# Seven of eight column groups of an up-projection by Strassen's seven block products

## The chip, the core and the metric

The kernel runs on one core of a Trainium2 chip. Its engines work side by side, each through its own queue in order: TensorE (PE, with its weight loads listed as PEld), VectorE (DVE), ScalarE (ACT), GpSimd (POOL) and SyncE (SP, which issues most transfers). Transfers run on the core's 16 DMA engines. The metric is the device time of one launch in microseconds.

## The reference

Two transformer blocks are computed for 256 tokens in float32, one after the other. The changed part is the feed-forward part of the first block:

```python
u = rms_norm(h, norm_mlp_w[l])                                    # 256 x 2048
h = h + jnp.square(jax.nn.relu(u @ w_up[l])) @ w_down[l]          # w_up 2048 x 8192, w_down 8192 x 2048
```

Before it stands a mixer (w_in, two kinds of attention, two branch projections, w_out), behind it a norm and the second block (w_in_2, two more kinds of attention, w_out_2).

## The kernel before

Every projection is a `Job`: 512 columns of one weight matrix times all 256 tokens, with two accumulators in PSUM, one for each half of the tokens (128 rows). TensorE multiplies in the fast format fp32r. To keep float32 accuracy each operand is split in two: a high part, rounded to fp32r, and a low part, the rest. Three of the four products are added: high x high, high x low, low x high. The activations lie transposed in `op_` tiles (`ops[name, g]`: two parts, 4 k tiles of 128, 256 tokens and 16 more columns), for `v` (the normed input of w_up) four tiles, for `h0` to `h3` (the squared relu of 2048 columns of w_up each) four tiles each. `xpose_split` makes them: four transposes on TensorE into a PSUM tile `sp`, the high part on ScalarE (L119), the low part on VectorE (L120), twice per tile.

`run_stream` is the loop over all weights. It cuts each job into pieces of 4 k tiles (512 rows of the weight, 1 MB, `raw`, three buffers) and each piece into two halves. `issue` loads a piece by SP (L241); `prep_hi` makes the high part `wh` of a half on ScalarE (L261, four buffers), three halves ahead; `prep_lo` the low part `wl` on VectorE (L275, three buffers), two halves ahead, and after a piece's second half issues the load that takes its buffer. `multiply` (L295; L293 for jobs with keys) then runs 12 matmuls of 512 columns for a half: two k tiles, two token halves, three products. At a job's last half `evac` empties the accumulators. Generators in `post` and `bg` hold the rest of the work (splits, scans, attention), and `gap` lets them go on by a step in the middle and at the end of each half. Nothing is reordered: each engine executes in the order in which this code is written.

For the feed-forward part 16 jobs of w_up and 16 of w_down alternate in groups of four: four of w_up make `h{q}`, four of w_down add its product to the residual `xres` (tiles `res`). `ev_up` takes relu on ScalarE, with the token's norm factor `r2` as scale (L721), and squares on VectorE (L722). `ev_down` adds to `res` on VectorE (L730). During the last group of w_up `prep2` loads and prepares the tables of the second block.

Of the kernel before, what the change touches and what calls it, by code (L numbers as in the profile page):

```python
# [8 lines left out]
F32 = mybir.dt.float32  # L9
F32R = mybir.dt.float32r  # L10
# [11 lines left out]
HI_AHEAD, LO_AHEAD, N_HI, N_LO = 3, 2, 4, 3  # L22
# [5 lines left out]
def two_blocks_kernel(  # L28
# [27 lines left out]
    raw_p = ctx.enter_context(tc.tile_pool(name="raw", bufs=3))  # L56
# [73 lines left out]
    def xpose_split(src, name, g, colscale=None, one=None):  # L130
# [74 lines left out]

    class Job:
# [3 lines left out]
        def __init__(self, w, r0, c0, name, groups, evac, keys=False):  # L210
            self.w, self.r0, self.c0, self.name = w, r0, c0, name
            self.groups = list(range(groups)) if isinstance(groups, int) else groups
            self.evac, self.keys = evac, keys
            self.nk, self.nc = (8, 256) if keys else (4, NCH)

        def pieces(self):
            if self.keys:
                return [(self, g * 512, ((g, range(4)), (g + 1, range(4)))) for g in self.groups[::2]]
            return [(self, g * 512, ((g, (0, 1)), (g, (2, 3)))) for g in self.groups]

    jobs = []

    def run_stream():
        pieces = [p for j in jobs for p in j.pieces()]
        halves = [(pi, h) for pi in range(len(pieces)) for h in range(2)]
        raws, whl = {}, {}

        def issue(pi, between=None):
            if pi >= len(pieces):
                return  # L230
            j, r, _ = pieces[pi]
            t = raw_p.tile([P, j.nk, j.nc], F32, tag="raw", name=nm("raw"))
            src = j.w[j.r0 + r:j.r0 + r + j.nk * P, j.c0:j.c0 + j.nc].rearrange("(k p) c -> p k c", p=P)
            if pi == 0:
                cuts = (0, 1, 2, 4)
            elif pi == 1:
                cuts = (0, 2, 4)
            else:
                cuts = (0, j.nk)
            for a, b in zip(cuts, cuts[1:]):  # L240
                nc.sync.dma_start(out=t[:, a:b, :], in_=src[:, a:b, :])  # L241
                if between is not None:
                    between(b)
            raws[pi] = t

        def half_of(i):
            pi, h = halves[i]
            j = pieces[pi][0]
            n = j.nk // 2
            return j, raws[pi][:, n * h:n * h + n, :]  # L250

        def prep_hi(i):
            if i >= len(halves):
                return
            j, t = half_of(i)
            wh = wh_p.tile([P, j.nk // 2, j.nc], F32R, tag="wh", name=nm("wh"))
            for k in ((0, 1), (1, 2)) if i < 2 else ((0, j.nk // 2),):
# [6 lines left out]
        def prep_lo(i):  # L264
            if i >= len(halves):
                return
            pi, h = halves[i]
            j, t = half_of(i)
            wh = whl[i][0]
            wl = whl[i][1] = wl_p.tile([P, j.nk // 2, j.nc], F32R, tag="wl", name=nm("wl"))  # L270
            for k in ((0, 1), (1, 2)) if i < 2 else ((0, j.nk // 2),):
# [4 lines left out]
            if h == 1:  # L276
                del raws[pi]
                issue(pi + 3)
                if 2 <= pi < 6:
                    load_x(pi - 2)  # L280

        def multiply(i, acc, t, kk):

            (pi, h), (wh, wl) = halves[i], whl[i]
            j, _, parts = pieces[pi]
            g, kts = parts[h]
            xt, k = ops[j.name, g], kts.index(kk)
            sl = slice(t * P, (t + 1) * P)
# [1009 lines left out]
```

## Time and profile before

| | |
|---|---|
| median of 3 runs | 1949.76 us (1949.54 to 1949.89) |
| profiled execution | 1949.31 us, of which the span from first to last instruction is 1947.5 us |
| TensorE | 1933.1 us busy, 99%, 9456 matmuls |
| VectorE | 1092.6 us, 56% |
| ScalarE | 899.6 us, 46% |
| GpSimd | 49.1 us, 3% |
| DMA | 344.88 MB, mean 177 GB/s |

TensorE's matmuls are pipelined, so one is listed with some 395 ns although the next starts some 232 ns later; the distance between starts is what counts. VectorE and ScalarE instructions that follow one another directly overlap a little too. "Idle before" an instruction is put down to what ended that wait. Where one transfer waits for a buffer, the queue of the engine that issues it is listed (SPq).

### The profile page before, as it was taken

The numbers are of one execution on the slowest core, as the hardware profiler recorded it, in microseconds if no ns is written. First come the engines' busy times: TensorE is split into PE (matmuls) and PEld (weight loads), VectorE is DVE, ScalarE is ACT, GpSimd is POOL, SyncE is SP. The second block draws the span as 40 slices with busy tenths as digits, with TensorE's granted clock in tenths as the row PEclk, the third lists the DMA queues.
The fourth block names the chain that finished last, engine by engine and source line by source line (L and its number), as shares of the span: only waits on it lengthen the run. The fifth ranks groups of instructions, "written<-read, shape, count | busy, mean of one in ns | idle before, by whom it ended". The sixth has DMA issues, their size and how long they took to land.

```text
span 1947.5 us, 23970 instructions
## 1 busy us (share of the span) xinstructions
PE 1933.1 (99%) x9456; PEld 1592.7 (82%) x9456; DVE 1092.6 (56%) x1526; ACT 899.6 (46%) x1267; POOL 49.1 (3%) x85
## 2 busy tenths in 40 slices
PE   9999999999999999999999999999999999999997
PEld 7888887878888888888888888888888999978886
DVE  5666655554446655555555545545566566666554
ACT  6444344364444445443444344435455444556542
POOL 0000010000000000000000000000000010001000
PEclk9999999999999999999999999999999999999999
DMA  8445464545555556555665665566555444444553
GB/s 311 152 153 170 153 197 159 173 148 180 184 191 184 184 180 195 176 192 182 187 196 183 195 182 185 186 184 211 177 188 179 159 151 136 140 151 149 176 180 123
DMA packets 183489, 344.88 MB, mean 177 GB/s; under 512 B 5888, under 2 KB 28416, under 8 KB 183376
## 3 DMA queue, kind: packets, MB, share of 16 engines
q1 hardware_dynamic: 180816, 336.48, 53.0%
q0 software_dynamic: 1696, 5.65, 0.9%
q8 instruction: 74, 1.21, 0.3%
q10 hardware_dynamic: 864, 1.21, 0.2%
q14 instruction: 39, 0.32, 0.0%
HBM read 341.23 MB, written 2.10 MB: 176 GB/s over the span
## 4 chain that ended last, share of the span: by engine, by line
PE 98%; DMA 1%; DVE 0%; ACT 0%; issue 0%; SPq 0%; DVEq 0%; POOLq 0%; POOL 0%; ACTq 0%
PE acc L295 84%; PE acc L293 6%; PE sp L142 2%; PE sp L501 1%; DMA raw<-in_w_in_dram 1%; PE sp L1090 1%; PE sp L1002 0%; PE sp L654 0%; PE sp L523 0%; PE sp L1042 0%; PE sp L1022 0%; PE sp L1023 0%; PE sp L1112 0%; PE sp L1111 0%; PE sp L667 0%
## 5 line engine op out<-in xcount | busy, mean ns | idle before, releaser
L275 DVE TENSOR_TENSOR wl<-raw,wh 128x1024 fp32r<-128x1024 f32 (+1 forms) x634 | 771.2, 1219 | 455.9 <-PE acc L295 370.9
L261 ACT ACTIVATE wh<-raw 128x1024 fp32r<-128x1024 f32 (+1 forms) x634 | 667.0, 1055 | 671.2 <-PE acc L295 634.9
L295 PE MATMUL acc<-wh,op_u 128*128 128x512 f32 x1408 | 463.2, 399 | 1.7 <-ACT wh L261 1.7
L295 PE MATMUL acc<-wh,op_v 128*128 128x512 f32 x1024 | 327.0, 395 | 0.0
L295 PE MATMUL acc<-wh,op_h 128*128 128x512 f32 x1024 | 324.0, 394 | 0.0
L295 PEld LDWEIGHTS acc<-wh,op_u 128*128 128x128 f32 x1408 | 264.4, 188 | 62.9 <-ACT wh L261 2.3
L295 PE MATMUL acc<-wl,op_u 128*128 128x512 f32 x704 | 277.8, 395 | 0.8 <-DVE wl L275 0.8
L295 PEld LDWEIGHTS acc<-wh,op_h 128*128 128x128 f32 x1024 | 192.3, 188 | 44.1
L295 PEld LDWEIGHTS acc<-wh,op_v 128*128 128x128 f32 x1024 | 192.3, 188 | 43.5
L295 PE MATMUL acc<-wl,op_h 128*128 128x512 f32 x512 | 201.8, 394 | 0.0
L295 PE MATMUL acc<-wl,op_v 128*128 128x512 f32 x512 | 201.7, 394 | 0.0
L295 PE MATMUL acc<-wh,op_z 128*128 128x512 f32 x512 | 177.0, 406 | 0.0
L295 PEld LDWEIGHTS acc<-wl,op_u 128*128 128x128 f32 x704 | 132.4, 188 | 29.7 <-DVE wl L275 2.5
L293 PE MATMUL acc<-op_z,wh 128*128 128x272 f32 x640 | 129.9, 295 | 0.0
L295 PEld LDWEIGHTS acc<-wh,op_z 128*128 128x128 f32 x512 | 96.2, 188 | 24.6 <-issue 4.3
L295 PEld LDWEIGHTS acc<-wl,op_h 128*128 128x128 f32 x512 | 96.1, 188 | 22.2
L295 PEld LDWEIGHTS acc<-wl,op_v 128*128 128x128 f32 x512 | 96.1, 188 | 21.7
L293 PEld LDWEIGHTS acc<-op_z,wh 128*128 128x128 f32 x640 | 102.4, 188 | 1.5 <-issue 1.1
L295 PE MATMUL acc<-wl,op_z 128*128 128x512 f32 x256 | 100.8, 394 | 0.0
L293 PE MATMUL acc<-op_z,wl 128*128 128x272 f32 x320 | 92.0, 288 | 0.0
L295 PE MATMUL acc<-wh,op_mg 128*128 128x512 f32 x256 | 82.1, 396 | 0.0
L295 PE MATMUL acc<-wh,op_y 128*128 128x512 f32 x256 | 80.6, 394 | 0.0
(264 smaller groups left out, 1664.6 us busy)
## 6 DMA issues: line engine op xcount, KB each, us to landing
raw<-in_w_in_dram SPq DMA_DIRECT2D x138, 1024.0 KB, 5.0
raw<-in_w_up_dram SPq DMA_DIRECT2D x64, 1024.0 KB, 5.5
raw<-in_w_down_dram SPq DMA_DIRECT2D x64, 1024.0 KB, 5.0
raw<-in_w_out_dram SPq DMA_DIRECT2D x32, 1024.0 KB, 5.0
raw<-in_w_branch_a_dram SPq DMA_DIRECT2D x8, 1024.0 KB, 5.1
raw<-in_w_branch_b_dram SPq DMA_DIRECT2D x8, 1024.0 KB, 5.1
res<-in_x_dram SPq DMA_DIRECT2D x4, 512.0 KB, 7.5
c<-in_relb_dram POOLq DMA_DIRECT2D x4, 512.0 KB, 5.7
```

Source lines behind the costliest of these rows:

```text
L142: nc.tensor.transpose(p[:, k, t * P:(t + 1) * P], src[:, t, c:c + P], ident_)
L261: act(out=wh[:, k], in_=t[:, k], func=AF.Copy)
L275: tt_(out=wl[:, k], in0=t[:, k], in1=wh[:, k].bitcast(F32), op=ALU.subtract)
L293: nc.tensor.matmul(acc, lhsT=b[:, k, sl], rhs=xt[:, a, kk, :], start=st, stop=en)
L295: nc.tensor.matmul(acc, lhsT=xt[:, a, kk, sl], rhs=b[:, k, :], start=st, stop=en)
L501: nc.tensor.matmul(p[:, 2 * h + t, :], lhsT=kq[:, h, s], rhs=qp[:, h, s], start=True, stop=True)
L1090: nc.tensor.matmul(p, lhsT=qT[64 * k:64 * k + 64, h, t * P:(t + 1) * P], rhs=kT[64 * k:64 * k + 64, h], start=True, stop=True)
```

## The change

The 8192 columns of w_up are eight units of 1024. Unit 0 is computed as before, by two jobs. For each unit from 1 to 7 the product of the 256 x 2048 input (2 x 2 blocks of 128 tokens by 1024 rows) and the unit's 2048 x 1024 weights (2 x 2 blocks b11, b12, b21, b22 of 1024 rows by 512 columns) is computed by seven block products in place of eight. Each product `p1` to `p7` has one accumulator and 8 k tiles, so four items (`Part`) of two k tiles and 6 matmuls.

The sums of activation blocks (`forms`) are made once, by `make_forms`, during unit 0: for p5, p6 and p3 in six own tiles of `c4`, and for p7 in place of a block of the `v` tiles that only unit 0 reads as it was. The sums of weight blocks are made for each item: b11 + b12 into a tile `sum` (VectorE, L342), and b12 + b22 in place (VectorE, L345). `sum` first serves p5 (as b11 + b12); when its low part is made, a DMA of POOL's queue adds b22 to it (L357), for p6; after p6 another adds b21, for p4. So b12, b22 and b21 are loaded twice. `finished` combines the products: p5, p1 and p7 are copied out of PSUM by ScalarE, the rest is added by VectorE from PSUM. `store_up` takes relu and square of the two finished 128 x 512 tiles, both on ScalarE, and appends the split.

The 28 product items of a unit alternate with the 16 w_down items of the unit before, in four rounds of `ppdppdppdpd` (p a product item, d a w_down item). w_down of unit 7 comes last, alone. A w_down job now has 1024 rows (four items) in place of 2048, 32 jobs in place of 16, and its two accumulators lie in the pool `sp`, because the products take the pool `acc`.

Loads are of two k tiles (512 KB) all through the kernel, six `raw` buffers in place of three of 1 MB, and each is issued when a buffer comes free, also after a block sum. Block sums are made four items ahead. `prep2` is split: half of it starts when unit 6 is stored, the other half (`prep2b`) when unit 7 is.

```diff
-HI_AHEAD, LO_AHEAD, N_HI, N_LO = 3, 2, 4, 3
+ADD_AHEAD, HI_AHEAD, LO_AHEAD, N_HI, N_LO, N_RAW = 4, 3, 2, 4, 3, 6
...
-    raw_p = ctx.enter_context(tc.tile_pool(name="raw", bufs=3))
+    raw_p = ctx.enter_context(tc.tile_pool(name="raw", bufs=N_RAW))
...
+        def begin(self):
+            if self.side:
+                self.accs = [ps([P, NCH]) for _ in range(2)]
+            else:
+                self.accs = [acc_p.tile([P, NKEY if self.keys else NCH], F32, tag="acc", name=nm("acc")) for _ in range(2)]
...
+    class Unit:
...
+        def items(self):
+            quarters = []
+            for names in (("p5", "p1"), ("p7", "p3"), ("p6",), ("p2",), ("p4",)):
+                for j in range(4):
+                    for n in names:
+                        quarters.append(Part(self, n, j))
+            return quarters
...
+        def finished(self, n):
+
+            a = self.bank.pop(n)
+            if n in ("p5", "p1", "p7"):
+                self.s[n] = w2([P, NCH])
+                nc.scalar.copy(out=self.s[n], in_=a)
+                return
+            s1, s5, s7 = (self.s[k] for k in ("p1", "p5", "p7"))
+            if n == "p3":
+                self.s[n] = w2([P, NCH])
+                tt_(out=self.s[n], in0=a, in1=s5, op=ALU.add)
+            elif n == "p6":
+                s6 = w2([P, NCH])
+                tt_(out=s6, in0=a, in1=s1, op=ALU.add)
+                tt_(out=s7, in0=s6, in1=s7, op=ALU.add)
+                tt_(out=s5, in0=s5, in1=s7, op=ALU.subtract)
+                tt_(out=self.s["p3"], in0=self.s["p3"], in1=s6, op=ALU.subtract)
+                self.store(1, (self.s["p3"], s5))
+            elif n == "p2":
+                tt_(out=s1, in0=a, in1=s1, op=ALU.add)
+            elif n == "p4":
+                tt_(out=s7, in0=a, in1=s7, op=ALU.add)
+                self.store(0, (s1, s7))
...
+        def adds(self):
+            u, j = self.unit, self.j
+            if self.n == "p5":
+                t = u.T["sum", j] = c4([P, 2, NCH])
+                tt_(out=t, in0=u.T["b11", j].t, in1=self.b12.t, op=ALU.add)
+                return 1
+            if self.n == "p7":
+                tt_(out=self.b12.t, in0=self.b12.t, in1=u.T["b22", j].t, op=ALU.add)
...
+        def prepared(self):
+            u, j = self.unit, self.j
+            if self.n in ("p5", "p6"):
+                more = u.load(1, 1 if self.n == "p5" else 0, j)
+                nc.gpsimd.dma_start(out=u.T["sum", j], in_=more.src, accum_op=ALU.add)
+                return 0
+            if self.n == "p4":
+                del u.T["sum", j]
+                return 0
+            return 1
...
+        def multiply(self, wh, wl):
+            u = self.unit
+            if self.j == 0:
+                u.bank[self.n] = acc_p.tile([P, NCH], F32, tag="acc", name=nm("acc"))
+            for k in range(2):
+                kt = 2 * self.j + k
+                for n, (a, w) in enumerate(((0, wh), (0, wl), (1, wh))):
+                    nc.tensor.matmul(u.bank[self.n], lhsT=form(u.name, self.n, a, kt), rhs=w[:, k, :],
+                                     start=kt == 0 and n == 0, stop=kt == 7 and n == 2)
...
+            prep_add(i + ADD_AHEAD)
             prep_hi(i + HI_AHEAD)
             prep_lo(i + LO_AHEAD)
...
+    def store_up(u):
+
+        def f(g, tiles):
+            for k, t in enumerate(tiles):
+                act(out=t, in_=t, func=AF.Relu, scale=r2[:, k:k + 1])
+                act(out=t, in_=t, func=AF.Square)
+            post.append(later(4, xpose_split([t.unsqueeze(1) for t in tiles], f"h{u}", g)))
+            if g == 0 and u >= 6:
+                bg.append(prep2() if u == 6 else prep2b())
+        return f
...
+    for u in range(1, 8):
+        parts, halves = deque(Unit(w_up, 1024 * u, "v", store_up(u)).items()), deque(down(u - 1))
+        for _ in range(4):
+            for kind in "ppdppdppdpd":
+                plan.append((parts if kind == "p" else halves).popleft())
+    plan.extend(down(7))
```

How instructions stand now is shown at three places; the number behind a name counts the tiles of that name. First TensorE inside a w_up job, before: one half item, two accumulators, 12 matmuls.

```order
L295 MATMUL acc1173_6892<-wh1167_6865,op_v1_908_5243 128x512
L295 MATMUL acc1173_6892<-wl1172_6890,op_v1_908_5243 128x512
L295 MATMUL acc1173_6892<-wh1167_6865,op_v1_908_5243 128x512 x2
L295 MATMUL acc1173_6892<-wl1172_6890,op_v1_908_5243 128x512
L295 MATMUL acc1173_6892<-wh1167_6865,op_v1_908_5243 128x512
L295 MATMUL acc1174_6893<-wh1167_6865,op_v1_908_5243 128x512
```

TensorE now, at the last item of p6 (L371, one accumulator, activations from the two parts `form1119` and `form1120`), with the w_down item behind it (L255, accumulator in `sp`):

```order
L371 MATMUL acc1555_7970<-wh1556_7977,form1119_5987 128x512
L371 MATMUL acc1555_7970<-wl1559_7990,form1119_5987 128x512
L371 MATMUL acc1555_7970<-wh1556_7977,form1120_5988 128x512
L371 MATMUL acc1555_7970<-wh1556_7977,form1119_5987 128x512
L371 MATMUL acc1555_7970<-wl1559_7990,form1119_5987 128x512
L371 MATMUL acc1555_7970<-wh1556_7977,form1120_5988 128x512
L255 MATMUL sp_1550_7950<-wh1558_7988,op_h20_1475_7615 128x512
L255 MATMUL sp_1550_7950<-wl1561_8007,op_h20_1475_7615 128x512
```

A pair `wh`, `wl` served 12 matmuls before and serves 6 in a product item. Second, VectorE at the end of a w_up job before: the square of both token halves (L722), then low parts.

```order
L275 TENSOR_TENSOR wl1002_5833<-raw985_5718,wh999_5815 128x1024
L722 TENSOR_TENSOR c4_1004_5849<-c4_1004_5849 128x512 x2
L275 TENSOR_TENSOR wl1006_5856<-raw993_5767,wh1001_5831 128x1024
L275 TENSOR_TENSOR wl1010_5874<-raw993_5767,wh1005_5854 128x1024
L120 TENSOR_TENSOR op_h01_1012_5890<-sp_1013_5891,op_h01_1012_5890 128x2x256
```

VectorE now, at the end of p6: its low parts (L490) of the next items stand before and behind the four combinations (L312 to L315), of which only the first reads PSUM.

```order
L490 TENSOR_TENSOR wl1561_8007<-raw1531_7860,wh1558_7988 128x1024
L490 TENSOR_TENSOR wl1564_8019<-raw1534_7872,wh1560_8005 128x1024
L312 TENSOR_TENSOR w2_1566_8029<-acc1555_7970,w2_1506_7764 128x512
L313 TENSOR_TENSOR w2_1544_7930<-w2_1566_8029,w2_1544_7930 128x512
L314 TENSOR_TENSOR w2_1499_7729<-w2_1499_7729,w2_1544_7930 128x512
L315 TENSOR_TENSOR w2_1547_7943<-w2_1547_7943,w2_1566_8029 128x512
L490 TENSOR_TENSOR wl1568_8040<-raw1537_7890,wh1563_8017 128x1024
L490 TENSOR_TENSOR wl1571_8058<-raw1540_7902,wh1567_8038 128x1024
```

And VectorE now at the end of a w_down job in the first round: the two sums into `res` (L958), directly behind them a block sum (L345), then low parts.

```order
L490 TENSOR_TENSOR wl1501_7733<-raw1479_7627,wh1496_7717 128x1024
L958 TENSOR_TENSOR res38_254<-sp_1473_7601,res38_254 128x512
L958 TENSOR_TENSOR res38_254<-sp_1474_7602,res38_254 128x512
L345 TENSOR_TENSOR raw1490_7679<-raw1490_7679,raw1495_7703 128x1024
L490 TENSOR_TENSOR wl1504_7754<-raw1487_7661,wh1500_7731 128x1024
```

Two instructions stood between low parts there before, and now up to four. Third, ScalarE, before at the end of a w_up job (relu straight from PSUM) and then now, at the end of p6 (relu L936 and square L937 of what VectorE combined):

```order
L261 ACTIVATE wh1167_6865<-raw1159_6801 128x1024
L721 ACTIVATE c4_1170_6883<-acc1150_6749,rstat_94 128x512
L721 ACTIVATE c4_1170_6883<-acc1151_6750,rstat_94 128x512
L261 ACTIVATE wh1171_6888<-raw1159_6801 128x1024
L261 ACTIVATE wh1175_6906<-raw1164_6835 128x1024
```

```order
L477 ACTIVATE wh1563_8017<-raw1537_7890 128x1024
L936 ACTIVATE w2_1547_7943<-w2_1547_7943,rstat_94 128x512
L937 ACTIVATE w2_1547_7943<-w2_1547_7943 128x512
L936 ACTIVATE w2_1499_7729<-w2_1499_7729,rstat_94 128x512
L937 ACTIVATE w2_1499_7729<-w2_1499_7729 128x512
L477 ACTIVATE wh1567_8038<-raw1540_7902 128x1024
L477 ACTIVATE wh1570_8056<-raw1543_7922 128x1024
```

The high part `wh1567`, of the fourth item after p6's last, now stands behind four instructions of which the first waits for VectorE's last combination.

## Rows read from the trace of the kernel before

**Rows 1.** The page: busy us (share of the span) and instructions by engine.

```profile
PE 1933.1 (99%) x9456; PEld 1592.7 (82%) x9456; DVE 1092.6 (56%) x1526; ACT 899.6 (46%) x1267; POOL 49.1 (3%) x85
```

**Rows 2.** TensorE's waits: for whom, us in total, times, longest.

```profile
PE acc L295 <- ACT wh L261: 1.7, 2, 1.2
PE sp L378 <- DVE mhalf L368: 1.1, 1, 1.1
PE acc L295 <- DVE wl L275: 0.8, 2, 0.4
```

**Rows 3.** The page: the chain that ended last, by engine.

```profile
PE 98%; DMA 1%; DVE 0%; ACT 0%; issue 0%; SPq 0%; DVEq 0%; POOLq 0%; POOL 0%; ACTq 0%
```

**Rows 4.** Windows over the feed-forward stage: busy us (instructions), granted clock, DMA share, GB/s.

```profile
core 0: us, PE busy (x) PEld busy (x) DVE busy (x) ACT busy (x) POOL busy (x), PEclk, DMA share, GB/s
692.00:783.00 91.00, 91.00 (x412) 74.07 (x411) 50.22 (x57) 45.26 (x61) 3.90 (x4) 1.00 0.58 183
...
1235.00:1326.00 91.00, 91.00 (x396) 73.76 (x395) 44.37 (x40) 35.24 (x34) 0.00 (x0) 1.00 0.59 187
1326.00:1416.00 90.00, 90.00 (x405) 73.14 (x405) 52.29 (x67) 46.81 (x63) 3.65 (x5) 1.00 0.60 197
sum 724.00, PE 724.00 PEld 588.08 DVE 382.56 ACT 321.54 POOL 9.69; mean PE 90.50 PEld 73.51 DVE 47.82 ACT 40.19 POOL 1.21
```

**Rows 5.** The chain in order of time, from 850 us: start, us, what.

```profile
853.88 0.44 PE sp L142 x4
854.31 108.41 PE acc L295 x468
```

**Rows 6.** Groups by line: busy us, mean ns | idle before.

```profile
L275 DVE TENSOR_TENSOR wl<-raw,wh 128x1024 fp32r<-128x1024 f32 x630 | 768.5, 1222 | 454.9 <-PE acc L295 370.9 <-issue 42.3 <-PE acc L293 22.6
L261 ACT ACTIVATE wh<-raw 128x1024 fp32r<-128x1024 f32 x630 | 664.5, 1058 | 670.4 <-PE acc L295 634.9 <-PE acc L293 30.8 <-DMA raw<-in_w_in_dram 2.5
L295 PEld LDWEIGHTS acc<-wh,op_v 128*128 128x128 f32 x1024 | 192.3, 188 | 43.5
L730 DVE TENSOR_TENSOR res<-acc,res 128x512 f32<-128x512 f32 x24 | 16.6, 692 | 12.4 <-PE acc L295 12.4
```

**Rows 7.** Timeline of VectorE, two places: start, us, instruction, idle before.

```profile
25.25 2.36 DVE L275 TENSOR_TENSOR wl<-raw,wh 128x1024 fp32r<-128x1024 f32 x2
...
890.49 0.69 DVE L730 TENSOR_TENSOR res<-acc,res 128x512 f32<-128x512 f32 x1 [0.70 <-PE acc L295]
891.10 1.22 DVE L275 TENSOR_TENSOR wl<-raw,wh 128x1024 fp32r<-128x1024 f32 x1
```

**Rows 8.** Timeline of ScalarE, two places.

```profile
23.98 3.12 ACT L261 ACTIVATE wh<-raw 128x1024 fp32r<-128x1024 f32 x3
...
798.91 0.69 ACT L721 ACTIVATE c<-acc,rstat 128x512 f32<-128x512 f32 x1 [0.70 <-PE acc L295]
799.49 1.05 ACT L261 ACTIVATE wh<-raw 128x1024 fp32r<-128x1024 f32 x1
```

**Rows 9.** DMA from 7 to 40 us: total, queue's share, issues with us to landing.

```profile
DMA packets 6789, 11.78 MB, mean 357 GB/s; under 512 B 263, under 2 KB 1825, under 8 KB 6788
q1 hardware_dynamic: 6788, 11.76, 100.4%
raw<-in_w_in_dram SPq DMA_DIRECT2D x7, 1024.0 KB, 7.5
```

**Rows 10.** DMA of the whole run: queues (packets, MB, share), issues.

```profile
q1 hardware_dynamic: 180816, 336.48, 53.0%
q0 software_dynamic: 1696, 5.65, 0.9%
raw<-in_w_up_dram SPq DMA_DIRECT2D x64, 1024.0 KB, 5.5
c<-in_relb_dram POOLq DMA_DIRECT2D x4, 512.0 KB, 5.7
```

**Rows 11.** SP's own waits.

```profile
SPq L241 <- DVE wl L275: 1624.2, 293, 10.8
```

**Rows 12.** Timeline of TensorE at the start.

```profile
10.21 0.73 PE L295 MATMUL acc<-wh,op_u 128*128 128x512 f32 x2 [1.20 <-ACT wh L261]
```

**Rows 13.** The window of the start, columns as in rows 4.

```profile
0.00:50.00 50.00, 46.43 (x195) 36.74 (x196) 29.02 (x48) 32.81 (x56) 2.17 (x7) 1.00 0.87 303
```

More of the change, by code (lines that the diff above doesn't have):

```diff
@@ L221, in two_blocks_kernel @@
-    jobs = []
-    def run_stream():
[L224 to L229, printed above, removed]
-                return
[L231 to L239, printed above, removed]
+            self.evac, self.keys, self.side = evac, keys, side
@@ L240, in issue @@
+    plan = []
+    def run_stream():
+        items = plan
+        loads = deque(l for it in items for l in it.loads)
+        whl = {}
+        def issue(between=None):
+            if not loads:
+                return
+            l = loads.popleft()
+            t = raw_p.tile(l.shape, F32, tag="raw", name=nm("raw"))
+            cuts = (0, 1, 2) if between is not None else (0, l.shape[1])
             for a, b in zip(cuts, cuts[1:]):
-                nc.sync.dma_start(out=t[:, a:b, :], in_=src[:, a:b, :])
+                nc.sync.dma_start(out=t[:, a:b, :], in_=l.src[:, a:b, :])
@@ L242, in issue, with prep_add, cuts_of @@
                 if between is not None:
                     between(b)
[L244 to L250, printed above, removed]
+            l.t = t
+        def prep_add(i):
+            if i < len(items):
+                for _ in range(items[i].adds() or 0):
+                    issue()
+        def cuts_of(i):
+            return ((0, 1), (1, 2)) if i < 2 else ((0, items[i].nk),)
@@ L252, in prep_hi @@
         def prep_hi(i):
[L253 removed]
+            if i >= len(items):
                 return
[L255 to L257 removed]
+            it = items[i]
+            t = it.src()
+            wh = wh_p.tile([P, it.nk, it.nc], F32R, tag="wh", name=nm("wh"))
+            for k in cuts_of(i):
                 if i < 8:
@@ L264, in prep_lo @@
         def prep_lo(i):
-            if i >= len(halves):
+            if i >= len(items):
                 return
[L267 to L271, printed above, removed]
+            it = items[i]
+            t, wh = it.src(), whl[i][0]
+            wl = whl[i][1] = wl_p.tile([P, it.nk, it.nc], F32R, tag="wl", name=nm("wl"))
+            for k in cuts_of(i):
                 if i < 8:
@@ L275, in prep_lo @@
                 tt_(out=wl[:, k], in0=t[:, k], in1=wh[:, k].bitcast(F32), op=ALU.subtract)
[L276 to L288, printed above, removed]
-            for n, (a, b) in enumerate(((0, wh), (1, wh), (0, wl)) if i < 2 else ((0, wh), (0, wl), (1, wh))):
-                st = g == j.groups[0] and kk == 0 and n == 0
-                en = g == j.groups[-1] and kk == 3 and n == 2
-                if j.keys:
-                    nc.tensor.matmul(acc, lhsT=b[:, k, sl], rhs=xt[:, a, kk, :], start=st, stop=en)
-                else:
-                    nc.tensor.matmul(acc, lhsT=xt[:, a, kk, sl], rhs=b[:, k, :], start=st, stop=en)
+            for _ in range(it.prepared()):
+                issue()
+            if i in (5, 7, 9, 11):
+                load_x((i - 5) // 2)
         start(issue)
+        for i in range(ADD_AHEAD):
+            prep_add(i)
         for i in range(HI_AHEAD):
```

256 lines of the change are left out of this document (195 added, 61 removed).

## The prediction

> **What bounds the kernel now.** I read the busy shares first, then what TensorE waits for, then the chain, then the stage that is changed. TensorE is busy 99% of the span [rows 1]. All its listed waits for another engine come to 3.6 us of 1947.5 [rows 2], and the chain that ended last is 98% TensorE [rows 3]. In the eight pairs of windows over the w_up and w_down stage TensorE is busy without a gap while VectorE works 53% (48 of 90 us), ScalarE 44% and the DMA engines about 59% of the time at 183 to 197 GB/s in the rows shown, with the granted clock at 1.00, the 2.4 GHz level [rows 4]. So the time here is the number of matmuls times their pace, and every other engine has room. The pace: 468 matmuls of 512 columns took 108.41 us [rows 5], 231.6 ns each. Four transposes take 0.44 us [rows 5]. The profiled execution took 1949.3 us (span 1947.5); the median of the runs is 1949.8, so I sum against 1949.3 and the half microsecond is within the rounding.
>
> **What is removed.** A unit of 1024 columns of w_up had 16 (k tiles) x 2 (column halves) x 2 (token halves) x 3 (high/low products) = 192 matmuls; seven block products of 8 k tiles x 3 are 168. Seven units lose 24 each: 168 matmuls x 0.2316 = **38.9 us**. The order of instructions bears it out: 9045 matmuls and transposes before, 8877 now, with all 168 among those of 512 columns. The weight loads go with their matmuls (188 ns, beside them [rows 6]). Nothing is added on TensorE: same transposes (16 per unit). The unit with its w_down items is then 360 x 0.2316 + 16 x 0.11 = 85.1 us, where the same work took 384 x 0.2316 + 1.8 = 90.7.
>
> The Trainium skill (TensorE: Matmul & The Clock Gate, "Back-to-back issue gap") puts 512 columns at N/2.4 + 2.5 = 216 ns; by that the gain would be 36.3 us. The trace shows 231.6, and that counts.
>
> **What VectorE and ScalarE gain.** A product item (two k tiles, one token half) gives TensorE 6 matmuls, 1.39 us, a w_down item 12, 2.78 us; but each needs a full 128x1024 subtraction on VectorE and a full 128x1024 copy on ScalarE. Durations are 1222 and 1058 ns [rows 6], yet back to back VectorE starts the next 1.14 us later (2.36 us for two, less 1.22) and 0.61 us after a 512-wide one (890.49 to 891.10) [rows 7]; ScalarE takes about 1.03 (3.12 for three) and 0.6 [rows 8]. Per unit VectorE has 44 subtractions and 8 block sums (nearest row: the subtraction of the same shape) = 52 x 1.14 = 59.3, and 8 w_down sums into res, 7 combinations of products, 4 splits of h = 19 x 0.61 = 11.6; together 70.9 of 85.1 us, **83%** (by full durations 76.7, 90%). ScalarE: 44 x 1.03 + 15 x 0.6 = 54.3, 64%. Neither becomes the bound on the mean, but VectorE runs in order, and three buffers of low parts let it lead TensorE by two items only. So I look where its queue is held by a wait on TensorE (T is the end of the item waited for; a first read of the bank comes 0.2 us after it [rows 7], and an item needs its low part 0.23 us after its start):
> - End of a w_down job in round one: second sum into res T+0.20, block sum for p7 T+0.81, subtraction for the item three ahead T+1.95 to 3.17. Two products lie between: needed at 2.78 + 0.23 = 3.01. **0.2 us** lost. Without the block sum (the other three rounds) it ends at 2.03: nothing.
> - End of p6: three dependent 0.69 us combinations and a fourth, done at T+2.9. Its items' own low part comes at T+4.1, due at 4.4: covered. But ScalarE has two relu and two squares queued ahead of the next high part: 2.9 + 4 x 0.6 = 5.3, high part 6.3, low part 7.6; due at 2.78 + 1.39 + 2.78 + 0.23 = 7.18. With some 0.06 us for each of six hand-overs **0.4 to 0.8**, I take 0.6; the tail (sum into res and h split behind it) another 0.1.
> - p3, p2 and p4 end with one combination, 0.6 us, and at least 2.8 us follow: nothing.
>
> That is 0.9 us per unit, x 7 = **6.3 us** (0 if hand-overs overlap, 14 if the durations rather than the spacings rule). The forms (13 VectorE instructions, 12.9 us) run in unit 0, whose 16 items of 2.78 us leave VectorE some 21 us; three of its steps wait for ScalarE. I add **1 us**, for that once.
>
> **What the DMA gains.** Per unit 36 loads of 512 KB instead of 32 (20 + 16), and 8 adding DMAs from POOL's queue: 23.1 MB in 85.1 us, 271 GB/s where there were 187. What a load costs the 16 engines: in the first 40 us they were busy throughout at 357 GB/s [rows 9], 1.47 us per load; in this stage 59% busy at 187 GB/s [rows 4], 1.65 us. An adding DMA is nowhere in the trace. Below, it costs what a plain one on that queue does: 5.65 MB took 0.9% of 1947.5 us [rows 10], 1.63 us (by the faster pace 1.5); above no row bounds it; it must also read its destination, so I take twice, 3.3, as the end of the range and 2.4 as value. On the mean 36 x 1.56 + 8 x 2.4 = 75 of 85 us. But the demand is bunched. Loads are issued when VectorE frees a buffer (SP waits for that [rows 11]), six buffers in all; from the start of a unit until its last p7 block sum is due, 18 items, 12 x 1.39 + 6 x 2.78 + 0.9 = 34.3 us, 16 loads are still to come and four adding DMAs: 29.5 us at the low prices, 39.6 at the high, 34.6 at mine. So DMA and TensorE run level there, and a load that is late stops VectorE in a block sum. The tightest load (second operand of a block sum) is issued 5.56 us of items ahead, less the 1.2 us of the operation that frees its buffer; 1 MB landed in 5.5 us alone [rows 10] and 7.5 under saturation [rows 9]. I take 1 us per unit, **7 us** (0 to 5.3 per unit, 37).
>
> The adding DMA itself is not on the path: from p5's subtraction to p6's high part lie 19 to 24 items (37 to 46 us), from p6 to p4 11 or 12 (some 21 us); the nearest 512 KB load on that queue landed in 5.7 us [rows 10].
>
> The Trainium skill (DMA: Bandwidth & Descriptors, "Anatomy of one DMA") fits 2.0 us + bytes/436 GB/s for DMAs of that path, 1.2 us of it movement here. By that figure the DMA term is nothing and the time 1918; no run here shows an adding DMA yet.
>
> Start and end: loads of 512 KB in place of 1 MB carry the same bytes in nearly the same order, with the saturated start [rows 9] as it was; plus or minus 1 us. The w_in_2 half and the tail keep their order.
>
> **Sum.** 1949.3 - 38.9 + 6.3 + 1 + 7 = 1924.7, so **1925 us**, a gain of 1.3%. Less than 0.2% (3.9 us) a measurement of this kernel can't tell from no change.
>
> **Rivals.**
> - *All covered.* VectorE's spacing has 17% of slack and the adding DMA is no dearer than a plain one. Only the 38.9 us count, perhaps a few lost: 1911 to 1916. For it: a low part that is late by 0.2 to 0.6 us is within what I can't resolve. Against: two engines near their mean bounds at once.
> - *VectorE becomes the bound.* If its instructions keep their full 1.22 and 0.69 us, because they wait for one another's results, ScalarE or a load, 76.7 us plus about four waits of 1.5 us per unit gives 83 to 88 us per unit: 1930 to 1945. For it: full durations are what single instructions show [rows 6]. Against: back-to-back rows [rows 7].
> - *The adding DMA is slow: no gain or slower.* It shares the 16 engines with the loads (queue shares in [rows 10] are of the same 16). Above 3.5 us each (38.9/7 - 0.9 = 4.7 us of stall per unit eat the gain: 34.3 + 4.7 = 39.0; less 16 x 1.56 leaves 14.0 for four) the change loses. At 4.0 us it is 41.0 against 34.3, 6.7 x 7 = 47 lost: 1949.3 - 38.9 + 7.3 + 47 = 1965. For it: read, add and write-back per byte. Against: nothing but the byte count, which gives 3.3 at most.
> - *Fewer matmuls in name only.* The order shows them gone, and nothing in their place; no chance.
>
> **How the numbers follow.** Forecast (1917 to 1934) 0.60, all covered 0.15, VectorE bound 0.10, slow adding DMA 0.15, of which 0.10 ends slower, 0.04 within 0.2% and 0.01 faster. Faster 0.86, same 0.04, slower 0.10. Range: from 1911, where nothing is lost, to 1946, where the DMA's high price is paid; about 0.14 lies above and little below.
>
> **What would show it.** Matmuls of 512 columns still 231 to 232 ns apart, 168 fewer. TensorE idle before the low part (wl) of the fourth item after p6's last, about 0.6 us, once per unit, and some 0.2 us at the first w_down job's end. DMA share in the stage near 0.9 in the first half of a unit and 0.7 in the second. If VectorE's block sums wait for a raw load, the DMA term is it; if TensorE waits for wl while VectorE has no idle time, VectorE is the bound. Waits of about 1 us leave the clock alone: TensorE's 1.20 us wait before 10.21 us [rows 12] lies in a window with granted clock 1.00 [rows 13]. I am wrong if an adding DMA holds the engines above 3.5 us, or if VectorE's instructions grow longer beside it.

## The result and the profile after

The changed kernel takes **1968.81 us** (median of 4 runs, 1966.93 to 1969.71) beside 1949.69 us (1949.54 to 1949.89) of the kernel before: 1.0097 times as long, 95% interval 1.0084 to 1.011. I had forecast 1925 us, in a range of 1911 to 1946; the time lies 44 us above the forecast, on the other side of no change.

The page of the changed kernel, busy time by engine and the chain that ended last (as [rows 1, 3]):

```profile
PE 1914.9 (97%) x9288; PEld 1565.8 (80%) x9288; DVE 1289.3 (66%) x1736; ACT 1012.8 (51%) x1405; POOL 116.0 (6%) x141
...
PE 89%; DMA 4%; DVE 3%; ACT 2%; issue 2%; DVEq 0%; POOL 0%; SPq 0%; POOLq 0%; ACTq 0%
```

TensorE runs 168 instructions fewer, as forecast, yet the chain is no longer TensorE alone: 98% have become 89%, and loads and VectorE have come into it. What TensorE waits for (us in total, times, longest; as [rows 2]):

```profile
PE acc L371 <- DVE wl L490: 18.3, 14, 3.9
PE sp L255 <- DVE wl L490: 15.6, 15, 2.2
PE acc L255 <- DVE wl L490: 3.6, 3, 2.0
```

So it waits for the low part `wl`, 37.5 us instead of 0.8. VectorE, which makes it, waits in its turn, in the block sums (L342 is b11 + b12 for p5, L345 is b12 + b22 for p7), for loads of w_up. The last row comes back in the last experiment:

```profile
DVE raw L345 <- DMA raw<-in_w_up_dram: 44.5, 26, 3.4
DVE c L342 <- DMA raw<-in_w_up_dram: 25.3, 13, 3.9
...
DVE res L977 <- DMA w<-in_norm_final_dram: 3.2, 1, 3.2
```

Together 69.8 us in 39 waits, five or six in each of seven units: always at p5's last two block sums and at p7's four. Windows of the stage (as [rows 4]: us, busy PE, PEld, DVE, ACT, POOL, granted clock, DMA share, GB/s):

```profile
800.00:900.00 100.00, 94.01 (x408) 74.76 (x407) 78.47 (x78) 58.55 (x65) 10.71 (x9) 0.98 0.89 249
900.00:1000.00 100.00, 93.55 (x403) 74.52 (x401) 77.60 (x77) 57.54 (x63) 10.73 (x9) 0.98 0.90 254
1000.00:1100.00 100.00, 94.61 (x405) 75.34 (x406) 78.35 (x78) 58.67 (x65) 10.75 (x9) 0.98 0.91 254
1100.00:1200.00 100.00, 96.06 (x403) 75.62 (x402) 78.35 (x78) 57.77 (x64) 9.54 (x8) 0.97 0.88 249
1200.00:1300.00 100.00, 94.61 (x412) 75.07 (x411) 78.82 (x77) 57.94 (x63) 9.54 (x8) 1.00 0.88 254
1300.00:1400.00 100.00, 93.71 (x403) 74.50 (x402) 77.45 (x82) 59.03 (x65) 11.89 (x11) 0.98 0.88 249
1400.00:1500.00 100.00, 95.44 (x418) 76.23 (x418) 71.92 (x92) 62.77 (x95) 10.60 (x13) 0.98 0.70 209
```

Before, TensorE had no gap here and the clock stood at 1.00. Now it is idle for 38.0 of these 700 us, and the clock, short of 1.00 by 0.02 to 0.03 in six of seven windows, takes about 12 us more (13 by the two digits of the windows; 12 by the clock record of the trace, which has seven falls to the lower level here). The kernel needs 38.9 + 19.1 = 58 us more than its matmuls at the old pace; these two are 50 of them.

**The loop.** The chain in order of time shows what the waits are made of (start, us, what):

```profile
982.13 1.23 DVE c L342
...
983.37 5.65 DMA raw<-in_w_up_dram
...
989.11 1.23 DVE c L342
...
990.36 7.35 DMA raw<-in_w_up_dram
...
997.80 0.09 DVE c L342
...
998.94 1.23 DVE wl L490
```

A block sum ends and frees a buffer; the load that takes the buffer lands 5.65 us later; the next block sum had waited for this very load; and again, 7.35 us. A turn is thus 1.2 + 5.7 to 7.4 = 7 to 8.7 us. In program order three items lie between two such sums, two products and a w_down half, at the least: 2 x 1.39 + 2.78 = 5.56 us. Each turn is late by 1.4 to 3.1 us, and two of them use up VectorE's lead. For the last three of p7's sums the buffer is freed not by a block sum but by a low part that stands behind one in VectorE's queue; a late block sum delays it as well, and the program leaves 5.56 to 6.95 us there. The end of that stretch, in the timeline (start, us, instruction, in brackets the idle time before it):

```profile
997.43 0.39 PE L371 MATMUL acc<-wh,op_v 128*128 128x512 f32 x1
997.80 1.22 DVE L342 TENSOR_TENSOR c<-raw,raw 128x1024 f32<-128x1024 f32 x1 [2.87 <-DMA raw<-in_w_up_dram]
...
1000.22 0.50 PE L371 MATMUL acc<-wl,op_v 128*128 128x512 f32 x1 [2.39 <-DVE wl L490]
...
1001.13 0.63 PE L371 MATMUL acc<-wl,op_v 128*128 128x512 f32 x1
...
1001.56 0.63 PE L371 MATMUL acc<-wh,op_v 128*128 128x512 f32 x1
1001.98 0.63 PE L255 MATMUL sp<-wh,op_h 128*128 128x512 f32 x1
```

TensorE stands for 2.39 us, and then the matmuls start 0.42 us apart instead of 0.23: the clock has fallen to its lower level, 1.2 GHz. The five-us windows about it (columns as above) show it, with the DMA engines full:

```profile
995.00:1000.00 5.00, 2.82 (x13) 1.97 (x11) 2.20 (x2) 0.86 (x1) 1.20 (x1) 1.00 1.02 287
1000.00:1005.00 5.00, 4.79 (x14) 3.79 (x15) 2.64 (x4) 2.20 (x3) 1.19 (x1) 0.66 1.01 313
```

**The price of an adding DMA.** DMA queues (packets, MB, share) and issues (KB each, us to landing), as [rows 10]:

```profile
q1 hardware_dynamic: 193456, 351.19, 56.1%
q0 software_dynamic: 16928, 35.02, 9.9%
...
raw<-in_w_up_dram SPq DMA_DIRECT2D x156, 512.0 KB, 4.8
...
c<-in_w_up_dram POOLq DMA_DIRECT2D x56, 512.0 KB, 8.3
```

POOL's queue holds the engines for 9.9% of 1966.7 us = 194.7 us; without the adding DMAs (first experiment, 1.0% of 1929.7) it is 19.3. So one adding DMA costs 175.4 / 56 = **3.13 us** of the 16 engines.

### The profile page after: what moved, and what is told of

Its sections match the earlier page's. It is cut to its first block, busy times and chain, and to the rows that moved or that the text cites. A ratio compares the mean times of both kernels' runs of the same rounds, so it can differ in the third digit from the quotient of the medians.

```text
span 1966.7 us, 25266 instructions
## 1 busy us (share of the span) xinstructions
PE 1914.9 (97%) x9288; PEld 1565.8 (80%) x9288; DVE 1289.3 (66%) x1736; ACT 1012.8 (51%) x1405; POOL 116.0 (6%) x141
## 3 DMA queue, kind: packets, MB, share of 16 engines
q0 software_dynamic: 16928, 35.02, 9.9%
## 4 chain that ended last, share of the span: by engine, by line
PE 89%; DMA 4%; DVE 3%; ACT 2%; issue 2%; DVEq 0%; POOL 0%; SPq 0%; POOLq 0%; ACTq 0%
PE acc L255 51%; PE sp L255 13%; PE acc L371 11%; PE acc L253 6%; DMA raw<-in_w_up_dram 3%; DVE wl L490 2%; PE sp L143 1%; PE sp L715 1%; DVE c L342 1%; PE sp L1322 1%; ACT wh L477 1%; ACT w L936 0%; DMA raw<-in_w_in_dram 0%; PE sp L1234 0%; PE sp L868 0%
## 5 line engine op out<-in xcount | busy, mean ns | idle before, releaser
L490 DVE TENSOR_TENSOR wl<-raw,wh 128x1024 fp32r<-128x1024 f32 (+1 forms) x634 | 763.7, 1216 | 287.4 <-PE acc L255 171.6
L255 PE MATMUL acc<-wh,op_u 128*128 128x512 f32 x1408 | 463.3, 400 | 1.7 <-ACT wh L477 1.6
L255 PEld LDWEIGHTS acc<-wh,op_u 128*128 128x128 f32 x1408 | 264.4, 188 | 63.2 <-ACT wh L477 2.8
L255 PE MATMUL sp<-wh,op_h 128*128 128x512 f32 x896 | 304.1, 401 | 0.0
L255 PE MATMUL acc<-wl,op_u 128*128 128x512 f32 x704 | 277.8, 395 | 0.4 <-DVE wl L490 0.4
L255 PEld LDWEIGHTS sp<-wh,op_h 128*128 128x128 f32 x896 | 171.6, 192 | 39.1
L255 PE MATMUL sp<-wl,op_h 128*128 128x512 f32 x448 | 181.3, 405 | 15.8 <-DVE wl L490 15.6
L255 PE MATMUL acc<-wh,op_z 128*128 128x512 f32 x512 | 176.6, 406 | 0.0
L371 PE MATMUL acc<-wh,op_v 128*128 128x512 f32 x448 | 157.7, 400 | 0.0
L255 PEld LDWEIGHTS acc<-wl,op_u 128*128 128x128 f32 x704 | 132.4, 188 | 29.3 <-DVE wl L490 2.1
L477 ACT ACTIVATE wh<-c 128x1024 fp32r<-128x1024 f32 x84 | 89.0, 1059 | 75.0 <-PE sp L255 43.8
L255 PEld LDWEIGHTS sp<-wl,op_h 128*128 128x128 f32 x448 | 85.7, 191 | 43.8 <-DVE wl L490 24.4
L371 PE MATMUL acc<-wh,form 128*128 128x512 f32 x336 | 116.5, 394 | 0.0
L255 PEld LDWEIGHTS acc<-wh,op_z 128*128 128x128 f32 x512 | 96.2, 188 | 24.9 <-issue 4.7
L371 PE MATMUL acc<-wl,op_v 128*128 128x512 f32 x224 | 90.7, 405 | 18.3 <-DVE wl L490 18.3
L490 DVE TENSOR_TENSOR wl<-c,wh 128x1024 fp32r<-128x1024 f32 x84 | 101.7, 1218 | 7.9 <-PE sp L255 5.7
L357 POOL DMA_DIRECT2D c<-in_w_up_dram x56 | 66.9, 1194 | 588.7 <-DVE wl L490 538.3
L255 PE MATMUL acc<-wl,op_z 128*128 128x512 f32 x256 | 100.7, 394 | 0.0
L371 PEld LDWEIGHTS acc<-wh,op_v 128*128 128x128 f32 x448 | 85.3, 190 | 18.4
```

What stands on the lines that cost most here:

```text
L255: nc.tensor.matmul(acc, lhsT=xt[:, a, kk, sl], rhs=b[:, k, :], start=st, stop=en)
L357: nc.gpsimd.dma_start(out=u.T["sum", j], in_=more.src, accum_op=ALU.add)
L371: nc.tensor.matmul(u.bank[self.n], lhsT=form(u.name, self.n, a, kt), rhs=w[:, k, :], start=kt == 0 and n == 0, stop=kt == 7 and n == 2)
L477: act(out=wh[:, k], in_=t[:, k], func=AF.Copy)
L490: tt_(out=wl[:, k], in0=t[:, k], in1=wh[:, k].bitcast(F32), op=ALU.subtract)
```

## The experiments

The theory after the result (A): the loop from a block sum over the freed buffer to the next load is longer than the work that covers it, and the adding DMAs lengthen it because they hold the engines that the loads need. The rivals: the engines' mean throughput in the stage, the bytes and the queue whatever the DMAs do, VectorE's own work. The "lead" of a load below is the TensorE time of the items between the instruction that frees its buffer and the point where it must have landed, counted in the order of the program, for the tightest load of a unit.

### The adding DMAs left out

```diff
-                more = u.load(1, 1 if self.n == "p5" else 0, j)
-                nc.gpsimd.dma_start(out=u.T["sum", j], in_=more.src, accum_op=ALU.add)
```

> The 56 adding DMAs are left out, so p6 and p4 multiply the wrong block sums; every other instruction stays. Theory A (late loads: a block sum frees a buffer, the next load starts, and the adding DMAs, 3.16 us of all 16 engines each, stretch that load from about 4 to 5.7 to 7.4 us, past the 5.56 us of items that cover it): the waits of the block sums L342 and L345 for raw loads (69.8 us in the changed kernel) fall below 10, the stage ends some 45 us earlier, time 1915 to 1927 us. Theory B (six buffers are too few whatever else loads): waits remain at half or more, time 1945 to 1960. Theory C (VectorE's queue is the bound): time within 10 us of the changed kernel's 1969.

The sums for p6 and p4 lack their further blocks here. Measured: **1931.62 us** (1931.43 to 1931.84; 0.9908 of before, 0.9893 to 0.9923). The adding DMAs cost 37.2 us in this order of the program, which is most of the loss, but the time lies 4.6 us above what theory A allowed: also without them VectorE waits for loads, 20 times, in the block sums for p7:

```profile
DVE raw L345 <- DMA raw<-in_w_up_dram: 29.7, 20, 2.3
```

VectorE's own instructions are the same as in the changed kernel, so its own work was not the bound (theory C).

### The same DMAs, plain

```diff
-                nc.gpsimd.dma_start(out=u.T["sum", j], in_=more.src, accum_op=ALU.add)
+                nc.gpsimd.dma_start(out=u.T["sum", j], in_=more.src)
```

> The same 56 DMAs on the same queue, but as plain loads that overwrite the sum instead of adding to it (p6 and p4 multiply b22 and b21 alone). This keeps bytes from memory, queue and waits, and takes away only the adding. Theory A with the adding as the cost: share of the software queue falls from 9.9% to about 5.5% (1.6 us for each 512 KB), time between e1 and the changed kernel, 1922 to 1940 us. If the extra bytes or the queue alone did it: 1955 to 1970.

The same bytes on the same queue overwrite instead of being added (so nothing is summed for p6 and p4). Measured: **1948.61 us** (1946.46 to 1952.54; 0.9999, 0.9989 to 1.0008). About half of the 37 us is the adding (20.2), half the mere presence of 56 more transfers (17.0); their bytes and their queue were not told apart. It fell between the two expectations, 8.6 us above the one and 6.4 below the other, so both have a part in it. The price of one, from the page:

```profile
q0 software_dynamic: 9760, 35.02, 5.7%
```

5.7% of 1946.1 us less 19.3 is 91.6, 1.64 us each, about half of the adding one's 3.13.

### Buffers held for less time

```diff
-ADD_AHEAD, HI_AHEAD, LO_AHEAD, N_HI, N_LO, N_RAW = 4, 3, 2, 4, 3, 6
+ADD_AHEAD, HI_AHEAD, LO_AHEAD, N_HI, N_LO, N_RAW = 3, 3, 2, 4, 3, 6
...
-            for names in (("p5", "p1"), ("p7", "p3"), ("p6",), ("p2",), ("p4",)):
+            for names in (("p1", "p5"), ("p3", "p7"), ("p6",), ("p2",), ("p4",)):
```

(In the part not shown the two loads of a block sum go with the item that uses them first: b11 with p1, b22 with p3, b12 with p5 and p7.)

> The adding DMAs stay. The first product of each pair now uses the block as loaded (p1 before p5, p3 before p7), and block sums are made three items ahead instead of four, so buffers are held shorter and the tightest load is issued 8.3 us of items ahead instead of 5.56. The result is complete. Theory A: loads of 5.7 to 7.4 us are mostly covered, time 1927 to 1945 us. Theory B: the same or better, 1920 to 1935. Theory C: no change, 1960 to 1970. If the 16 engines' total is the bound (0.90 busy): 1945 to 1960.

Everything is computed as in the changed kernel, adding DMAs included. Measured: **1932.15 us** (1931.07 to 1935.68; 0.9914, 0.9899 to 0.9928), a gain of 36.7 us over it. VectorE's waits for loads are 12.0 us in place of 69.8:

```profile
DVE raw L343 <- DMA raw<-in_w_up_dram: 10.1, 8, 2.1
...
DVE c L340 <- DMA raw<-in_w_up_dram: 1.9, 4, 0.6
```

The same window in the changed kernel and in this one (columns as above):

```profile
830.00:1400.00 570.00, 541.97 (x2320) 431.14 (x2319) 446.45 (x443) 333.57 (x364) 59.61 (x51) 0.98 0.89 251
```

```profile
830.00:1400.00 570.00, 560.14 (x2456) 450.07 (x2455) 480.45 (x472) 353.39 (x388) 66.72 (x59) 1.00 0.93 268
```

The DMA engines are busier (0.93 against 0.89) and TensorE is idle for 9.9 us in place of 28.0. So the engines' mean throughput was not what stopped the changed kernel. The w_up loads even landed later here (median 5.2 us against 4.8), and the time fell all the same.

What is left is of another kind. Six waits, 9.3 of the 12.0 us, stand at p7's second block sum, whose two loads are issued 9.7 and 12.5 us of items ahead. One of them, in the chain (start, us, what):

```profile
905.25 11.41 DMA raw<-in_w_up_dram
...
916.68 0.04 DVE raw L343
```

This load took 11.41 us, in a stretch in which the DMA engines are full. About the first and the second half of that unit (columns as above):

```profile
887.00:930.00 43.00, 41.99 (x185) 33.64 (x184) 37.66 (x35) 25.50 (x28) 4.77 (x4) 1.00 0.98 293
930.00:973.00 43.00, 42.43 (x189) 34.18 (x187) 34.26 (x36) 26.89 (x30) 4.80 (x4) 1.00 0.85 233
```

So the time to landing is not a constant that a lead can simply be set against: it was 5.65 and 7.35 us in the loop of the changed kernel and 11.41 us here.

### Buffers held for less time, adding DMAs left out

The two edits above together; the sums for p6 and p4 lack their further blocks.

> Both edits: shorter holds and no adding DMAs (p6 and p4 multiply the wrong block sums). Theories A and B: what remains is the wait after p6 (0.6 us per unit) and little else, 1913 to 1923 us. Theory C: 1955 or more.

Measured: **1924.55 us** (1923.93 to 1925.33; 0.9872, 0.9857 to 0.9886), 1.6 us above the range. With the loop covered the adding DMAs cost 7.6 us (1932.15 less 1924.55), where they cost 37.2 before. Without them VectorE's waits for w_up loads are 0.5 us; those at p7's second sum are gone.

### Each half of that edit alone

Block sums three items ahead instead of four, in the old order of the parts:

```diff
-ADD_AHEAD, HI_AHEAD, LO_AHEAD, N_HI, N_LO, N_RAW = 4, 3, 2, 4, 3, 6
+ADD_AHEAD, HI_AHEAD, LO_AHEAD, N_HI, N_LO, N_RAW = 3, 3, 2, 4, 3, 6
```

> Only the constant changes: the block sums are made three items ahead of their matmuls instead of four; the order of the parts stays that of the changed kernel. Counted in the order of the program, a weight load at its tightest has then 6.95 us of items between the instruction that frees its buffer and the item that must have it, against 5.56 us in the changed kernel (1968.8 us) and 8.34 us in the kernel with the parts swapped as well (1932.2 us). Theory A (the loop block sum, freed buffer, load is longer than the work that covers it): the loop measured 7 to 8.7 us in the changed kernel, so most but not all of its 37 us over the swapped kernel goes: 1935 to 1955 us, with DVE waits on w_up loads between 10 and 70 us. Rival B (the order of the parts was what helped, since the swapped order asks for loads one by one): 1962 to 1970 us. Rival C (the earlier sums alone did the harm): 1930 to 1934 us.

Measured: **1948.34 us** (1946.52 to 1952.54; 0.9997, 0.9987 to 1.0006). And the parts swapped, with their loads as above, and sums four items ahead:

```diff
-            for names in (("p5", "p1"), ("p7", "p3"), ("p6",), ("p2",), ("p4",)):
+            for names in (("p1", "p5"), ("p3", "p7"), ("p6",), ("p2",), ("p4",)):
```

> The other half alone: parts swapped (p1 before p5, p3 before p7), sums four items ahead as in the changed kernel. Tightest load 6.95 us of items, the same as with the constant alone, but four such loads in a unit instead of five or six. Theory A (cover of the load loop): 1934 to 1952 us, within some 10 us of the kernel with the constant alone. Rival B (the order of the parts is what helped): 1930 to 1935 us. Rival C (the earlier sums alone did the harm): 1962 to 1970 us.

Measured: **1941.49 us** (1940.11 to 1942.25; 0.9959, 0.9944 to 0.9974). Both fall where the lead puts them, and neither half does it alone: rivals B and C are out in both runs. All runs so far side by side, sums of VectorE's waits for w_up loads (L342 and L345, or the same lines two up) and of TensorE's for `wl` in us:

| kernel | lead | added DMAs | VectorE waits | TensorE waits | median |
|---|---|---|---|---|---|
| changed | 5.56 | 56 adding | 69.8 | 37.5 | 1968.8 |
| plain DMAs | 5.56 | 56 plain | 53.7 | 25.6 | 1948.6 |
| none added | 5.56 | 0 | 29.7 | 12.3 | 1931.6 |
| sums later | 6.95 | 56 adding | 37.4 | 23.8 | 1948.3 |
| parts swapped | 6.95 | 56 adding | 34.1 | 20.3 | 1941.5 |
| both | 8.34 | 56 adding | 12.0 | 13.6 | 1932.2 |
| both, none added | 8.34 | 0 | 0.5 | 8.5 | 1924.6 |

Down the table with all 56 adding DMAs, a longer lead is a shorter time; at one lead, fewer or cheaper transfers are. The two kernels with 6.95 us differ by 6.9 us; they have six and four loads of that lead in a unit, by the count in program order alone. The lead orders the kernels, but it does not say which load is late: with the sums later p7's third sum, one of whose loads has 6.95 us, waits 0.2 us in all, and the first two, with 8.34, up to 3.0 us at a time. That stays open. More buffers, or the adding DMAs at another time with the loads as they are, were not tried.

### The end of p6 spread

The two experiments that follow start from the kernel with both halves (1932.15 us). Only the sum that frees p6's bank stays in one piece; the other three sums and relu and square are issued by a step per item (relu and square at the end of p4 too; that part of the edit is not shown):

```diff
-                tt_(out=s7, in0=s6, in1=s7, op=ALU.add)
-                tt_(out=s5, in0=s5, in1=s7, op=ALU.subtract)
-                tt_(out=self.s["p3"], in0=self.s["p3"], in1=s6, op=ALU.subtract)
-                self.store(1, (self.s["p3"], s5))
+                s3 = self.s["p3"]
+                self.store(1, (s3, s5), (lambda: tt_(out=s7, in0=s6, in1=s7, op=ALU.add),
+                                         lambda: tt_(out=s5, in0=s5, in1=s7, op=ALU.subtract),
+                                         lambda: tt_(out=s3, in0=s3, in1=s6, op=ALU.subtract)))
```

> The kernel with the swapped parts and the shorter lead (1932.2 us), and with the end of p6 spread: only the sum that frees the bank stands in one piece, the three other sums and the relu and squares are issued one step to an item behind. Theory A (the wait of about 0.6 us behind the end of p6, once a unit, is in TensorE's path as forecast): 8 waits on the residue line of the p parts, 4.4 us in all, go, and some of the 5.7 us on the w_down line: 1924 to 1929 us. Rival B (the time of that wait is given back at the next load, the loads being the bound now): 1930 to 1934 us. Rival C (the spread pieces push later conversions back): 1935 us or more.

Measured: **1926.20 us** (1924.64 to 1928.24; 0.9883, 0.9867 to 0.9899). 6.0 us go, in theory A's range. TensorE's waits in the products' line, before the edit and after it:

```profile
PE acc L369 <- DVE wl L488: 4.4, 8, 0.6
```

```profile
PE acc L369 <- DVE wl L488: 0.4, 1, 0.4
```

These listed waits fall by 4.0 us, and the 5.7 us on the w_down line, of which I expected some to go, stay. The other 2 us stand in no listed wait; the runs of the two kernels spread over 4.6 and 3.6 us.

### norm_final loaded ahead

In every kernel with the Strassen units VectorE waits 3.2 to 3.5 us once, at the first w_down job after unit 7, for the weights of the last norm. GpSimd's timeline in the kernel before, and in the kernel with the end of p6 spread:

```profile
1342.01 1.49 POOL L820 TENSOR_TENSOR st<-sm,mhalf 16x1 f32<-16x1 f32 x1 [351.09 <-DVE sm L819]
1343.46 2.19 POOL L743 DMA_DIRECT2D w<-in_norm_final_dram  x4
```

```profile
1414.55 1.52 POOL L1066 TENSOR_TENSOR st<-sm,mhalf 16x1 f32<-16x1 f32 x1 [40.38 <-DVE sm L1065]
1416.04 2.18 POOL L976 DMA_DIRECT2D w<-in_norm_final_dram  x4
```

The load stands behind an operation of `prep2b` that waits for VectorE. That background work now starts a unit later than the rest of `prep2`, and so the load goes out at 1416 us, some 70 us later than before and just as it is needed. VectorE in that kernel, and what became of TensorE (window columns as above):

```profile
1421.18 1.29 DVE L982 TENSOR_TENSOR res<-res,w 128x512 f32<-128x512 f32 x2 [3.52 <-DMA w<-in_norm_final_dram]
```

```profile
1422.00:1426.00 4.00, 1.89 (x9) 1.18 (x8) 4.00 (x13) 3.81 (x8) 0.00 (x0) 0.90 0.04 15
1426.00:1430.00 4.00, 4.00 (x16) 3.18 (x15) 2.64 (x5) 1.42 (x2) 0.00 (x0) 0.68 0.74 250
```

The edit issues the first of the four loads before `prep2b`:

```diff
+            if g == 0 and u == 7:
+                wfs.append(load_wf(0))
             if g == 0 and u >= 6:
                 bg.append(prep2() if u == 6 else prep2b())
...
-            wf = w2([P, NCH])
-            nc.gpsimd.dma_start(out=wf, in_=norm_final[:, c * NCH:(c + 1) * NCH].broadcast_to([P, NCH]))
+            wf = wfs.pop() if wfs else load_wf(c)
```

> The kernel with swapped parts, the shorter lead and the spread end of p6 (1926.2 us), and the first of the four norm_final loads issued ahead of the background work that ends in a GpSimd operation; nothing else moves. In all kernels with the Strassen units so far that load is issued behind that GpSimd operation, VectorE waits 3.2 to 3.5 us for it, TensorE stands still for some 2.1 us behind it and then runs a stretch at a granted clock of 0.68 to 0.98; in the kernel before it is issued 70 us ahead and nobody waits. Theory A (the load stands behind the GpSimd operation): the wait on norm_final goes, no fall of the clock at the end of the seventh unit: 1920 to 1922 us. Rival B (VectorE is late there for other reasons, so the stop moves to the next item): 1924 to 1927 us. Rival C (the buffer that it holds longer is missed elsewhere): above 1927 us.

Measured: **1923.22 us** (1922.86 to 1923.49; 0.9865, 0.9849 to 0.9882). The wait is gone and TensorE runs through that place at a clock of 1.00, but 3.0 us come back where I expected 4 to 6: TensorE's waits on w_down's `wl` (L255, `sp`) are 6.8 us in place of 5.7, and those on `wh` 2.5 in place of 1.6. This is the best version that was run, 45.6 us below the changed kernel and 1.35% below the kernel before, which computes the same.

## Why the prediction was wrong

**What held.** 168 matmuls are gone at an unchanged pace. VectorE keeps its spacing when it has its data (three 1024-wide operations from 920.97 us in 3.49, as forecast 1.14 each), so it did not become the bound. The wait behind p6 is what I worked out, 0.6 us by way of ScalarE's queue; the timeline of the changed kernel:

```profile
956.81 0.68 DVE L315 TENSOR_TENSOR w<-w,w 128x512 f32<-128x512 f32 x1
...
957.53 0.73 ACT L936 ACTIVATE w<-w,rstat 128x512 f32<-128x512 f32 x1 [3.08 <-DVE w L315]
...
960.10 3.89 ACT L477 ACTIVATE wh<-raw 128x1024 fp32r<-128x1024 f32 x4
...
961.17 2.36 DVE L490 TENSOR_TENSOR wl<-raw,wh 128x1024 fp32r<-128x1024 f32 x2 [2.54 <-ACT wh L477]
...
962.46 0.50 PE L371 MATMUL acc<-wl,op_v 128*128 128x512 f32 x1 [0.57 <-DVE wl L490]
```

The relu, squares, high part and low part follow as in the prediction, and TensorE waits 0.57 us; the seven waits come to 4.0 us where I had 0.6 x 7 = 4.2. The rest of my 6.3 us is not borne out: the 0.2 us at the end of a w_down job stand in no listed wait of the kernel with covered loads and no adding DMAs. That 6.3 lies beside the 6.0 us that went with this end is in part luck.

**The step that failed: the DMA term.** I put it at 1 us per unit, 7 us in all. By the runs it is 44.3 us, 6.3 per unit (1968.81 less 1924.55, between the changed kernel and the one with covered loads and no adding DMAs; the falls of the clock behind late loads are in it). Four things were wrong in it.
- *The question.* I compared the engines' work in a stretch of 34.3 us with the length of that stretch, and wrote that "DMA and TensorE run level there". That model, at the measured 3.13 us and my 1.56 for a load, gives 16 x 1.56 + 4 x 3.13 = 37.5 us, 3.2 us lost per unit, 22 in all and a time of 1940, still faster. It hardly knows the order of the parts: swapping them moves the last block sum by one product, 1.39 us per unit and 10 us in all; the swap alone gave 27.3 us. What decides is each load's own way: freed buffer, issue, landing, against the work in between. Only with the loads covered is the first half of a unit about as full as the model had it (0.98). That the adding DMAs then cost 7.6 us, near my 7, is luck, since the model with the measured price says 22.
- *The number I had and did not use.* I wrote that the tightest load is issued 5.56 us of items ahead, less 1.2 us, that is 4.4 us, and that 1 MB landed in 5.5 us alone and 7.5 under saturation [rows 9, 10]. "Alone" was a misreading: [rows 10] is the median of the whole run. The loads of 512 KB in the loop landed in 5.65 and 7.35 us. I took 1 us of lateness in a unit, as if one load were late and the next on time; but VectorE waits for five or six loads in a unit, each turn of the loop is late again, and VectorE's lead of two items is spent once.
- *The price and the threshold.* 3.13 us for an adding DMA lies inside my bounds (1.5 to 3.3), though I took 2.4. The rival "slow adding DMA" was to decide above 3.5 us; the kernel lost at 3.13. The threshold came from the same model of a stretch, so the rival's mechanism was near and its condition wrong.
- *The range.* Its upper end, 1946, is not the sum with my own high price: 1949.3 - 38.9 + 6.3 + 1 + 37 = 1954.7. The time lies above that too.

By the Trainium skill (DMA: Bandwidth & Descriptors, "Anatomy of one DMA") I had estimated 1.2 us of movement for such a DMA: the trace has 1.64 us for the plain one and 3.13 for the adding one, and the measurement decides. The factor of 1.9 fits another page: Collectives: The Full Stack, "The bandwidth ceiling: the fold count and why AG ≠ RS ≠ AR", puts an adding transfer at about half the rate of a copying one, since two sources are read, not because the sum costs time; that page speaks of transfers between cores, and of the reads no run here shows anything.

**The clock.** "Waits of about 1 us leave the clock alone" was right where it was read, and not enough. Waits of 2.39 us (before the window at 0.66) and of 2.11 us (before the one at 0.68) were followed by a fall to the lower level. The seven falls in this stage of the changed kernel came behind waits of 1.76 to 3.87 us; but the length of one wait does not tell it, since of these two only the second was followed by a fall (granted clock 1.00 from 821 to 830 us, 0.72 from 1190 to 1196):

```profile
821.62 0.50 PE L255 MATMUL sp<-wl,op_h 128*128 128x512 f32 x1 [1.82 <-DVE wl L490]
...
1191.23 0.50 PE L255 MATMUL sp<-wl,op_h 128*128 128x512 f32 x1 [1.76 <-DVE wl L490]
```

The falls cost about 12 us in the changed kernel and nearly none with the loads covered (1.00 over 830 to 1400 us). No term of the sum held this.

**The tail.** I wrote that it keeps its order. On POOL's queue it does not: `prep2b` pushes the norm_final load 70 us back, worth 3.0 us.

**The account.** 1949.7 - 38.9 + 44.3 (loads) + 6.0 (end of p6) + 3.0 (norm_final) = 1964.1; 4.7 us of the 1968.8 are left. They hold the forms (1 us in the forecast) and other single waits, and I didn't split them. The 6.0 and the 3.0 were measured with the loads covered, so the sum supposes that they cost the same in the changed kernel.

## What to carry to other kernels

When a change raises the demand on a resource with few buffers, follow one buffer around: who frees it, when its load is issued, when it lands, who waits for that, and compare this turn with the work that lies between two of them. A mean share of 0.89 busy with room to spare says nothing about a loop that is too short. If it is, hold each buffer for less time (ask for it later, use it sooner) before making the transfers cheaper: here that gave back 36.7 of 44 us, without a byte less. And take the landing time from a stretch as full as the one that is planned: for the same 512 KB it was 5.65 us in one place and 11.41 in another.

## What the runs showed of the hardware

A DMA that adds to its destination held the 16 engines for 3.13 us per 512 KB, a plain one of the same queue and size for 1.64; its queue lists 128 more packets for each (16928 against 9760 for 56 DMAs). What 56 adding DMAs cost in time depended on the order of the program: 37.2 us with the loop uncovered, 7.6 with the loop covered. And seven stops of TensorE, of 1.76 to 3.87 us, were followed by a fall of the clock and so paid twice, first as idle time and then in matmuls 0.42 us apart instead of 0.23; one of 1.82 us was not.
